# A third slot for the stream of weights inside two feed-forward loops: every third load goes into a buffer that another tile calls home

## The chip, the cores and the metric

The kernel runs on one core of one Trainium2 chip. TensorE (PE) multiplies matrices, ScalarE (ACT) and VectorE (DVE) do elementwise work, GpSimd (POOL) issues some of the transfers, SyncE (SP) issues the rest. The metric is the time of one execution on the device, in microseconds; a time given for a kernel is the median over several executions, and a profile is one further execution with the hardware profiler on.

## The reference, cut to what matters

The kernel computes one decoder layer on 512 tokens of width 1024 in float32: a feed-forward part, a mixing part (attention and a linear recurrence side by side), a second feed-forward part. Each is wrapped in a norm before and a norm behind.

```python
def swiglu(x, w_gate, w_up, w_down):
    return (jax.nn.silu(x @ w_gate) * (x @ w_up)) @ w_down

f = swiglu(rms_norm(h, ffn1_norm_pre[l]), ffn1_w_gate[l], ffn1_w_up[l], ffn1_w_down[l])
h = h + 0.5 * rms_norm(f, ffn1_norm_post[l])
u = rms_norm(h, mix_norm_pre[l])
...                                   # attention, recurrence, their gates
h = h + rms_norm(merged @ w_out[l], mix_norm_post[l])
f = swiglu(rms_norm(h, ffn2_norm_pre[l]), ffn2_w_gate[l], ffn2_w_up[l], ffn2_w_down[l])
h = h + 0.5 * rms_norm(f, ffn2_norm_post[l])
```

The inner width of both feed-forward parts is 2816, that is 22 parts of 128 columns. Only these two parts (called ffn1 and ffn2 below) are touched.

## The kernel before, in words

**Numbers in two halves.** A float32 product is made of three matmuls on a reduced type, fp32r. Every operand is first split into a high part, which ScalarE writes as a copy into fp32r (L278), and a low part, which VectorE makes as the difference (L279). So each piece of weights passes a load, a ScalarE copy and a VectorE subtraction before TensorE can use it. The three matmuls of a triple are high by high, high by low and low by high (L603 to L605 in the feed-forward products; L397 to L399 where the product is turned towards tokens; L783 to L785 in `down7`).

**The stream of weights.** All weights lie in device memory in the order of use. `raw_of` (L217 to L234) hands them out by key; at the first key of a group it allocates a tile `raw` of 128 x 2048 float32 (1 MB) and issues one load on SyncE (L224). The tiles have two buffers (tag `raw`, `bufs=2`), so a load can start only when the last reader of the load two before it is done. There are 118 groups, numbered from 0; the first eight are loaded by `fetch_start`, the other 110 by L224.

**A feed-forward part.** The 22 parts of columns are cut into five blocks (4, 4, 4, 4 and 6 parts). The first few parts are computed plainly. For every later part f there is a `prep` (function `w_forms`) and a `prod`. `w_forms` loads gate and up weights of f as one group, `gu`, makes sums of its quarters on VectorE (L579, L580, L581, L584) and splits them into the seven operands of a Strassen-like scheme. `prod` (functions `seven` and `product`) runs seven products of twelve matmuls in the order p1, p2, p6, p5, p7, p4, p3; copies of the results go out on ScalarE (L610, tile `c`), and VectorE forms `u` and `g` from them (L615). A `Silu` on ScalarE (L724) and a multiplication on VectorE (L725) give the activation, which `into` splits for later use. The `prep` of part f+1 stands in the program before the `prod` of part f.

**The way down.** After each of the blocks 1, 2 and 3 the product with the down weights is taken by `down7`, again with seven products; each of its 14 results is copied by ScalarE into one of eight slices of a tile `cs` (L789), and GpSimd issues 16 transfers (L791) that add these slices to the accumulator `facc` in SBUF. `d_forms` loads the two groups `dg` for it. Block 0 goes through `down` in two halves (L713 to L720, copies out at L717), and block 4 through `last_product` (L416), which also applies the gain row of the norm behind and takes sums of squares. In ffn1 `last_product` puts the weights of its second half into tiles of the tags `xf`, `e` and `tx`, in ffn2 into three further tiles called `wide` (shown as `big` in the profile).

**Homes.** Tiles of the feed-forward pool share buffers by tag, one buffer each for those named here. Tag `wd`: the activation of part 3 of block 0 (`act3`), which the two halves of `down(0, ...)` read; after ffn's loop, the gain rows of the norms (`gains`, L408, loaded by GpSimd at L409). Tag `tt`: sums of activations for `down7` (`sevens[a]["tt"]`, written in `into`, L725 and L687). Tag `e`: the other activations of block 0 (`act`), then the tile `cs` of each `down7`, then one operand of ffn1's `last_product`.

**What sets the order.** The program text gives dependences; a scheduler that works on its own estimate of times decides the order of the instructions on each engine. `tc.high_priority(offset=...)` lets it move the enclosed lines ahead by that many places: `AHEAD` (100) is round the loads and splits of weights, `EVAC` (200) round the copies out and the sums in `seven` and `down7`. On the chip each engine runs its own instructions in the order so decided and waits with semaphores for the others.

Of the kernel before, what the change touches and what calls it, by code (L numbers as in the profile page):

```python
# [10 lines left out]
F32 = mybir.dt.float32  # L11
# [5 lines left out]
P = 128  # L17
# [12 lines left out]
RAW_W = 2048  # L30
# [47 lines left out]
def part_blocks(a):  # L78

    return (FF_PARTS[a][1] - FF_PARTS[a][0]) // 2  # L80
# [62 lines left out]
def stream_groups():  # L143

    groups, cur, w = [], [], 0
    for key, width in stream_plan():
        if w + width > RAW_W or (cur and cur[0][0][0] == "start"):
            groups.append(cur)
            cur, w = [], 0
        cur.append((key, w, width))  # L150
        w += width
    groups.append(cur)
    return groups
# [12 lines left out]
def hybrid_layer(ctx: ExitStack, tc: tile.TileContext, xT: bass.AP, xN: bass.AP, wst: bass.AP,  # L166
# [6 lines left out]
    wpool = ctx.enter_context(tc.tile_pool(name="wpool", bufs=4))  # L173
# [24 lines left out]
    def fb(b, sl=slice(0, D)):  # L198
        return facc[:, 2 * b:2 * b + 2, :].rearrange("p k t -> p (k t)")[:, sl]
# [10 lines left out]
    DVE.memset(eps, EPS)  # L210


    groups = stream_groups()
    state = {"g": 0, "i": 0, "off": 0, "raw": None, "ahead": AHEAD}

    def raw_of(key):

        g, i = state["g"], state["i"]
        grp = groups[g]
        if i == 0:  # L220
            w = grp[-1][1] + grp[-1][2]
            raw = wpool.tile([P, RAW_W], F32, name="raw", tag="raw", bufs=2)
            src = bass.AP(tensor=wst.tensor, offset=wst.offset + state["off"], ap=[[w, P], [1, w]])
            nc.sync.dma_start(raw[:, :w], src)  # L224
            state["raw"] = raw
            state["off"] += w * P
        k, o, w = grp[i]
        assert k == key, (k, key)
        src = state["raw"][:, o:o + w]
        if i + 1 == len(grp):  # L230
            state["g"], state["i"] = g + 1, 0
        else:
            state["i"] = i + 1
        return src  # L234

    def fetch(key, slot=None, ahead=0):

        with tc.high_priority(offset=ahead if slot else state["ahead"]):
            src = raw_of(key)
            w = src.shape[-1]  # L240
            t = slot() if slot else w8() if w > 512 else w4()
            split(t[:, 0, :w], t[:, 1, :w], src)
            return t[:, 0, :w], t[:, 1, :w]
# [37 lines left out]
    def acc_ps():  # L281
        return psum.tile([P, T], F32, name="acc", tag="acc", bufs=5)

    def aux_ps():
        return psum.tile([P, T], F32, name="aux", tag="aux", bufs=3)

    def tmp(name):
        return tpool.tile([P, T], F32, name=name, tag="t")
# [17 lines left out]
    def gemm(ps, wt, x, sl=slice(0, T), n=None):  # L306
        n = n or x.n
        a, b = k128(wt[0], n), k128(wt[1], n)
        for k in range(n):
            mm3(ps, a[:, k, :], b[:, k, :], x.hi[k][:, sl], x.lo[k][:, sl], k == 0, k == n - 1)  # L310
# [50 lines left out]
    def warm(acc):  # L361
        d = cpool.tile([P, 1], F32, name="warm", tag="warm")
        ACT.activation(d, acc[:, 0:1], AF.Abs_reciprocal_sqrt, bias=eps, scale=1.0 / D)
# [23 lines left out]
    def square(src):  # L387

        q, t = tmp("sq"), stat()
        ACT.activation(q, src, AF.Square, accum_out=t)  # L390
        return t

    def tokens(ps, ws, x, b, fill=lambda: None):
        bl = slice(b * P, (b + 1) * P)
        for k in range(x.n):
            wh, wl = (w.rearrange("p (k c) -> p k c", k=2)[:, k % 2, :] for w in ws[k // 2])
            PE.matmul(ps, x.hi[k][:, bl], wh, start=k == 0, stop=False)  # L397
            PE.matmul(ps, x.hi[k][:, bl], wl, start=False, stop=False)  # L398
            PE.matmul(ps, x.lo[k][:, bl], wh, start=False, stop=k == x.n - 1)  # L399
            if k == x.n // 2 - 1:  # L400
                fill()
# [11 lines left out]
    def last_product(key, nk, x, added, grow, slots, block, fills={}, apart=False):  # L413


        sums = {}  # L416
        warm(eps)
        for half, fs in enumerate(FHALVES):
            ws = [fetch(key(half, kk), slots.pop(0) if half else None) for kk in range(nk)]
            for b in range(4):  # L420
                ps = acc_ps()
                tokens(ps, ws, x, b, fills.get((half, b), lambda: None))
                src, y = ps, fb(b, fs)
                if added:
                    DVE.tensor_add(y, ps, y)
                    src = y
                sums[b, half] = square(src)
                z = tmp("z") if apart and half else y
                DVE.tensor_mul(z, src, grow[:, fs])
                if half:  # L430
                    block(b, (sums[b, 0], sums[b, 1]), *([z] if apart else []))

    class Boundary:
# [7 lines left out]
        def block(self, b, sums):  # L441
            r = root(sums, self.f)
            DVE.scalar_tensor_tensor(hb(b), fb(b), r, hb(b), op0=ALU.mult, op1=ALU.add)
            nc.gpsimd.dma_start(self.kept[b], hb(b))
            r = root([square(hb(b, fs)) for fs in FHALVES], 1.0)
            us = []
            for fs in FHALVES:
                u = tmp("u")
                DVE.scalar_tensor_tensor(u, hb(b, fs), r, self.grow[:, fs], op0=ALU.mult, op1=ALU.mult)
                us.append(u)  # L450
            self.u[b] = us
# [68 lines left out]
    def tx_slot(pool, bufs=1):  # L520
        return pool.tile([P, 2, 4, HB], F32R, name="tx", tag="tx", bufs=bufs)
# [46 lines left out]

        return t, [early, middle, late]

    spool = [None]

    def w_forms(key):

# [58 lines left out]
    def ffn(n, x, r, forms_x, apool, pss):  # L633
# [26 lines left out]
        def part(a):  # L660
            his, los = zip(*(acts["at", f] for f in range(*FF_PARTS[a])))
            return Act(his, los)
# [48 lines left out]
        def down(a, half):  # L711
            ws = [fetch(("down", n, a, half, kk)) for kk in range(part_blocks(a))]
            for b in range(4):  # L713
                ps, y = acc_ps(), fb(b, FHALVES[half])
                tokens(ps, ws, part(a), b)
                if a == 0:
                    ACT.activation(y, ps, AF.Copy)  # L717
                else:
                    DVE.tensor_add(y, ps, y)

        def prod(f, w):
            g, u = tmp("g"), tmp("u")
            seven(t, w, aux_ps()[:, :HB], [g[:, h] for h in HALVES], [u[:, h] for h in HALVES])
            ACT.activation(g, g, AF.Silu)  # L724
            into(f, lambda dst: DVE.scalar_tensor_tensor(dst, g, -1.0, u, op0=ALU.mult, op1=ALU.mult))  # L725
# [78 lines left out]
        for ev in ffn_order(n):  # L804
            if ev[0] == "std":
                j = ev[1]
                while len(pss) < 2 * j + 2:
                    pss.append(acc_ps())
                    gemm(pss[-1], fetch(keys[len(pss) - 1]), x)
                std_out(pss[2 * j], pss[2 * j + 1], j)  # L810
                if j < len(steps):
                    steps[j]()
            elif ev[0] == "prep":
                forms[ev[1]] = w_forms(("gu", n, ev[1]))
            elif ev[0] == "prepd":
                forms["d"] = d_forms(ev[1])
            elif ev[0] == "down":
                down(ev[1], ev[2])
            elif ev[0] == "down7":
                down7(ev[1], *forms.pop("d"))  # L820
            else:
                prod(ev[1], forms.pop(ev[1]))
        a = len(FF_PARTS) - 1
        return lambda half, kk: ("down", n, a, half, kk), part_blocks(a), part(a)

# [6 lines left out]
    def spare(pool):  # L832

        def of(t):
            return t[:, 0:4, :].rearrange("p (s k) t -> p s (k t)", s=2)

        return {"e": lambda: of(pool.tile([P, 8, T], F32R, name="act", tag="e", bufs=1)),
                "tt": lambda: of(pool.tile([P, 4, T], F32R, name="act", tag="tt", bufs=1)),
                "xf": lambda: of(pool.tile([P, 4, T], F32R, name="xf", tag="xf", bufs=4)),
                "tx": lambda: tx_slot(pool).rearrange("p s k t -> p s (k t)")}  # L840
# [14 lines left out]
    for k in range(KC):  # L855
        wh, wl, raw = wts[k]
# [9 lines left out]


    end1 = ffn(1, u1, r1, x_forms("g1a", r1, ap1), ap1, pss)
    new_h()
    for b in range(4):  # L870
# [10 lines left out]
            bd1.turn(b - 2)  # L881

    last_product(*end1, True, grow1, [spare(ap1)[i] for i in ("xf", "e", "tx")], block1)
    ff1.close()


    with ExitStack() as mx:
        tpl = mx.enter_context(tc.tile_pool(name="attn_out", bufs=1))
        apool_cm = tc.tile_pool(name="attention", bufs=1)
        apool = apool_cm.__enter__()  # L890
# [207 lines left out]
        for c in range(0, KC, 2):  # L1098
            g, u = tmp("g"), tmp("u")
# [308 lines left out]
```

## Time and profile before

| what | value |
|---|---|
| median of 3 executions | 1270.91 us (1269.04 to 1272.77) |
| the profiled execution's own time | 1275.29 us |
| its span in the profile | 1273.5 us |
| mean granted clock of TensorE | 0.987 |
| TensorE busy | 1230.8 us, 97% of the span |
| VectorE busy | 971.4 us, 76% |
| ScalarE busy | 735.1 us, 58% |
| loads at L224 | 110 of up to 1 MB, median 4.8 us from issue to landing |

A row of the timeline gives an instruction's start, its duration, engine, line and operation, written tile <- read tiles, and in brackets how long the engine sat idle before it and what released it. A row of waits gives the total time waited, the number of times and the longest. A row of a stretch gives, after the stretch's bounds and length, the busy time of PE, PE's weight loads, DVE, ACT and POOL with the number of instructions, then the granted clock, the mean busy share of the 16 DMA engines and GB/s. Lines below are of the kernel before.

In time, ffn1 lies in the first 350 us of the span, and ffn2's feed-forward loop in the last 340.

### The profile page before, as it was taken

Reading aid. Unit: us, or ns where it says so; the run is one execution under the profiler, and the core shown is the slowest. Engines: PE = TensorE matmul, PEld = TensorE weight load, DVE = VectorE, ACT = ScalarE, POOL = GpSimd, SP = SyncE. Lnnn points to the kernel's source line nnn. Section 1 sums busy time; section 2 is a strip of 40 time slices with the busy share of each in tenths; the row PEclk is TensorE's granted clock in tenths of the full one; section 3 lists DMA queues with packets and bytes.
Section 4 is the critical chain, followed back from the end, with each engine's and each line's share of the span. In section 5 each row is a group of like instructions: output and inputs, shape, how many; then the busy total and the mean of one; then the engine's idle time right before and its main releaser. Section 6 shows DMA issues by size and latency. Waiting matters only on the chain.

```text
span 1273.5 us, 19380 instructions
## 1 busy us (share of the span) xinstructions
PE 1230.8 (97%) x7676; PEld 1114.4 (88%) x7676; DVE 971.4 (76%) x1521; ACT 735.1 (58%) x1214; POOL 113.4 (9%) x153
## 2 busy tenths in 40 slices
PE   9999999999999999999999999999999999989887
PEld 8889888989777899999988887888998989888886
DVE  7969697878577488888575888854885879787855
ACT  7546656565455455666543797634664575756442
POOL 0000314030002000000000000000100031313000
PEclk9999999999899999999999999999999999999889
DMA  6233859584535122222242222225533386858631
GB/s 237 100 105 111 198 150 209 140 199 134 196 116 158 66 108 80 96 77 98 98 167 99 94 74 97 102 97 182 161 122 115 103 204 153 202 140 187 157 133 66
DMA packets 42075, 169.72 MB, mean 133 GB/s; under 512 B 4608, under 2 KB 7808, under 8 KB 27904
## 3 DMA queue, kind: packets, MB, share of 16 engines
q1 hardware_dynamic: 20016, 122.86, 28.0%
q0 software_dynamic: 21968, 45.62, 16.5%
q8 instruction: 60, 0.98, 0.3%
q14 instruction: 31, 0.25, 0.1%
HBM read 129.67 MB, written 6.29 MB: 107 GB/s over the span
## 4 chain that ended last, share of the span: by engine, by line
PE 73%; DVE 12%; DMA 8%; ACT 5%; issue 2%; DVEq 0%; SPq 0%; ACTq 0%
PE acc L603 8%; PE acc L604 8%; PE acc L605 8%; DMA raw<-in_w 8%; PE acc L291 6%; PE acc L292 6%; PE acc L293 6%; DVE w L279 4%; PE acc L397 3%; PE acc L399 3%; PE acc L398 3%; PE acc L783 2%; PE acc L784 2%; PE acc L785 2%; PE aux L603 2%; PE aux L604 2%
## 5 line engine op out<-in xcount | busy, mean ns | idle before, releaser
L279 DVE TENSOR_TENSOR w<-raw,w 128x1024 fp32r<-128x1024 f32 (+1 forms) x279 | 304.0, 1094 | 105.5 <-ACT w L278 93.1
L278 ACT ACTIVATE w<-raw 128x1024 fp32r<-128x1024 f32 (+1 forms) x279 | 265.5, 954 | 155.4 <-PE acc L293 48.3
L603 PE MATMUL acc<-big,w 128*128 128x256 f32 x896 | 254.7, 284 | 0.6 <-ACT c L610 0.6
L604 PE MATMUL acc<-big,w 128*128 128x256 f32 x896 | 254.6, 284 | 0.0
L605 PE MATMUL acc<-big,w 128*128 128x256 f32 x896 | 254.1, 284 | 0.0
L603 PEld LDWEIGHTS acc<-big,w 128*128 128x128 f32 x896 | 172.1, 192 | 1.4 <-ACT c L610 0.9
L604 PEld LDWEIGHTS acc<-big,w 128*128 128x128 f32 x896 | 172.0, 192 | 0.4
L605 PEld LDWEIGHTS acc<-big,w 128*128 128x128 f32 x896 | 172.0, 192 | 0.0
L603 PE MATMUL acc<-tx,w 128*128 128x256 f32 x272 | 80.0, 294 | 24.1 <-ACT c L610 23.9
L791 POOL DMA_DIRECT2D facc<-cs x96 | 82.0, 872 | 152.7 <-ACT cs L789 75.8
L610 ACT ACTIVATE c<-acc 128x256 f32<-128x256 f32 x172 | 65.0, 378 | 49.8 <-PE acc L605 46.1
L603 PE MATMUL aux<-big,w 128*128 128x256 f32 x288 | 83.2, 289 | 0.0
L604 PE MATMUL aux<-big,w 128*128 128x256 f32 x288 | 83.1, 288 | 0.0
L605 PE MATMUL aux<-big,w 128*128 128x256 f32 x288 | 83.0, 288 | 0.0
L605 PE MATMUL acc<-tx,w 128*128 128x256 f32 x272 | 78.7, 289 | 0.0
L604 PE MATMUL acc<-tx,w 128*128 128x256 f32 x272 | 78.4, 288 | 0.0
L603 PEld LDWEIGHTS acc<-tx,w 128*128 128x128 f32 x272 | 53.5, 197 | 26.5 <-ACT c L610 26.5
L291 PE MATMUL acc<-big,w 128*128 128x512 f32 x192 | 74.7, 389 | 0.0
L292 PE MATMUL acc<-big,w 128*128 128x512 f32 x192 | 74.7, 389 | 0.0
L293 PE MATMUL acc<-big,w 128*128 128x512 f32 x192 | 74.7, 389 | 0.0
L579 DVE TENSOR_TENSOR s<-raw 128x512 f32<-128x512 f32 x52 | 35.9, 690 | 47.0 <-DMA raw<-in_w 46.9
L279 DVE TENSOR_TENSOR w<-s,w 128x1024 fp32r<-128x1024 f32 x52 | 63.5, 1221 | 2.8 <-ACT w L278 2.7
(352 smaller groups left out, 2982.7 us busy)
## 6 DMA issues: line engine op xcount, KB each, us to landing
raw<-in_w SPq DMA_DIRECT2D x110, 1024.0 KB, 4.8
facc<-cs POOLq DMA_DIRECT2D x96, 256.0 KB, 6.7
raw<-raw POOLq DMA_DIRECT2D x6, 512.0 KB, 4.4
big<-xf POOLq DMA_DIRECT2D x6, 512.0 KB, 4.5
gains<-in_rows POOLq DMA_DIRECT2D x5, 512.0 KB, 7.4
h<-in_x SPq DMA_DIRECT2D x8, 256.0 KB, 5.2
h<-in_xn POOLq DMA_DIRECT2D x4, 512.0 KB, 5.5
kept_m<-h POOLq DMA_DIRECT2D x4, 512.0 KB, 2.9
```

The lines of the kernel that those rows point to most:

```text
L278: ACT.activation(dh, src, AF.Copy)
L279: DVE.tensor_sub(dl, src, dh.bitcast(F32))
L291: PE.matmul(ps, wh, xh, start=first, stop=False)
L292: PE.matmul(ps, wh, xl, start=False, stop=False)
L293: PE.matmul(ps, wl, xh, start=False, stop=last)
L397: PE.matmul(ps, x.hi[k][:, bl], wh, start=k == 0, stop=False)
L398: PE.matmul(ps, x.hi[k][:, bl], wl, start=False, stop=False)
L603: PE.matmul(ps, wh, xh, start=start and k == 0, stop=False, skip_group_check=True)
L604: PE.matmul(ps, wh, xl, start=False, stop=False, skip_group_check=True)
L605: PE.matmul(ps, wl, xh, start=False, stop=k == 3, skip_group_check=True)
L610: ACT.activation(c, ps, AF.Copy)
L791: nc.gpsimd.dma_start(fb(o + i, FHALVES[half]), c, accum_op=ALU.add)
```

## The change

Group g of the stream is loaded into a third place when g divided by 3 leaves 2 and such a place is set. From the end of `down(0, 1)` on, the place is the buffer of tag `wd`; after the loop over ffn's events it is the buffer of tag `tt`; after ffn1's `last_product` it is none again, and `down(0, 0)` of ffn2 sets it to none too. The groups so placed are 14, 17, 20, 23, 26, 29, 32 and 35 (tag `wd`) and 38 (tag `tt`) in ffn1, and 92, 95, 98, 101, 104, 107, 110 and 113 (tag `wd`) and 116 (tag `tt`) in ffn2. Group 14 is `gu` of part 6, group 92 is `gu` of part 5. The list `spool`, of which only the first place was used before (the pool of the tag `s`), now has a second place and is made earlier.

```diff
--- before.py
+++ after.py
@@ -210,6 +210,7 @@
     DVE.memset(eps, EPS)
 
 
+    spool = [None, None]
     groups = stream_groups()
     state = {"g": 0, "i": 0, "off": 0, "raw": None, "ahead": AHEAD}
 
@@ -219,7 +220,10 @@
         grp = groups[g]
         if i == 0:
             w = grp[-1][1] + grp[-1][2]
-            raw = wpool.tile([P, RAW_W], F32, name="raw", tag="raw", bufs=2)
+            if spool[1] is not None and g % 3 == 2:
+                raw = spool[1][0].tile([P, RAW_W], F32, name="raw", tag=spool[1][1], bufs=1)
+            else:
+                raw = wpool.tile([P, RAW_W], F32, name="raw", tag="raw", bufs=2)
             src = bass.AP(tensor=wst.tensor, offset=wst.offset + state["off"], ap=[[w, P], [1, w]])
             nc.sync.dma_start(raw[:, :w], src)
             state["raw"] = raw
@@ -568,7 +572,6 @@
 
         return t, [early, middle, late]
 
-    spool = [None]
 
     def w_forms(key):
 
@@ -816,10 +819,12 @@
                 forms["d"] = d_forms(ev[1])
             elif ev[0] == "down":
                 down(ev[1], ev[2])
+                spool[1] = (apool, "wd") if ev[2] else None
             elif ev[0] == "down7":
                 down7(ev[1], *forms.pop("d"))
             else:
                 prod(ev[1], forms.pop(ev[1]))
+        spool[1] = apool, "tt"
         a = len(FF_PARTS) - 1
         return lambda half, kk: ("down", n, a, half, kk), part_blocks(a), part(a)
 
@@ -881,6 +886,7 @@
             bd1.turn(b - 2)
 
     last_product(*end1, True, grow1, [spare(ap1)[i] for i in ("xf", "e", "tx")], block1)
+    spool[1] = None
     ff1.close()
```

The loads are the same in number and size; the activation of part 3, the gain rows and the sums of activations keep their tags.

## The prediction, on record before the changed kernel ran

> **What bounds the kernel now.** I read the page's busy times first, then what ended TensorE's idle time, then the timeline at each of TensorE's gaps, back through ScalarE and VectorE to the load.
>
> ```profile
> span 1273.5 us, 19380 instructions
> PE 1230.8 (97%) x7676; PEld 1114.4 (88%) x7676; DVE 971.4 (76%) x1521; ACT 735.1 (58%) x1214; POOL 113.4 (9%) x153
> raw<-in_w SPq DMA_DIRECT2D x110, 1024.0 KB, 4.8
> facc<-cs POOLq DMA_DIRECT2D x96, 256.0 KB, 6.7
> PE acc L603 <- ACT c L610: 24.5, 11, 3.7
> PE acc L397 <- ACT xf L278: 6.3, 2, 3.2
> DVE s L579 <- DMA raw<-in_w: 46.9, 28, 3.8
> ```
>
> TensorE is the bound: 1230.8 of 1273.5 us. Two groups hold 24.5 + 6.3 = 30.8 us of its 42.7 idle: thirteen gaps, all in the feed-forward loops. The profiled run took 1275.29 us, 4.4 above the median 1270.91; the sum is made against 1275.29 and carried to the median at the end.
>
> What makes a typical gap, after a `down7` (times are starts; brackets give idle time and releaser):
>
> ```profile
> 148.52 0.33 SPq L224 DMA_DIRECT2D raw<-in_w  x1
> DMA to landing us min/median/max: 7.6/7.6/7.6
> 156.17 0.69 DVE L579 TENSOR_TENSOR s<-raw 128x512 f32<-128x512 f32 x1 [3.40 <-DMA raw<-in_w]
> 161.49 0.63 ACT L724 ACTIVATE g<-g 128x512 f32<-128x512 f32 x1 [4.18 <-DVE g L615]
> 162.45 0.39 PE L603 MATMUL acc<-tx,w 128*128 128x256 f32 x1 [3.07 <-ACT c L610]
> 163.00:165.00 2.00, 2.00 (x19) 2.00 (x18) 2.00 (x5) 1.57 (x3) 0.00 (x0) 1.00 0.97 233
> 97.24 0.39 PE L603 MATMUL acc<-tx,w 128*128 128x256 f32 x1 [1.48 <-ACT c L610]
> 289.77 0.39 PE L603 MATMUL acc<-tx,w 128*128 128x256 f32 x1 [2.98 <-ACT c L610]
> 290.00:296.00 6.00, 6.00 (x39) 6.00 (x39) 4.41 (x8) 3.55 (x7) 0.00 (x0) 0.72 0.97 234
> ```
>
> A load that is issued at 148.52 and lands 7.6 us later holds VectorE's first sum of the next weights for 3.40 us. Behind it in VectorE's order stand the sums of the running product; behind these ScalarE's activation, then its copy, then TensorE. In the rows of stretches (busy time by engine, then granted clock, DMA share, GB/s) the mean clock is 1.00 behind this gap of 3.07, and 0.72 over the 6 us behind that of 2.98: 6 x 0.28 = 1.7 us lost. So a gap of this size sometimes also brings slow clock.
>
> [...]
>
> **The change part by part.** Loads are the same 110 and the same bytes, and every engine issues the same instructions; what moves is their order, slots and waits.
>
> *Ring of three, inner products (gaps after `down7`).* With two slots load n waits for the last reader of n−2. With every third load elsewhere it waits, in the built program, for that of n−2 or n−3, and since the loads go in order on SyncE, load n+1 takes the instant that load n had (148.52 brings the load after). VectorE's sums of that load are moved forward with it, to the same place ahead of the running product's sums. So VectorE waits again about 3.4 us, and the gap stays: seven gaps at 0, between −2 each if the load came early enough and +1 if more transfers collide. Only at 97.24 is there no `down7` beside it; there load 15 comes before its sums are due, and I take its 1.48 gap away: **−1.4** (0 to −1.5).
>
> *ffn1, third `down7`.* The load of the last half of the final `down` (load 38, slot `tt`) needs no ring slot and stands in the built SyncE order ahead of load 32, so it is issued at about 260. Its first split (ScalarE, L278 → `act`, into the buffers of tag `e`) now stands right behind the copy that began at 278.90. The tag `e` is also where `down7` keeps `cs`, the sources of its accumulating transfers, so that split waits for the last eight of these.
>
> ```profile
> 260.47 0.33 SPq L224 DMA_DIRECT2D raw<-in_w  x1
> 278.90 0.37 ACT L610 ACTIVATE c<-acc 128x256 f32<-128x256 f32 x1
> 279.91 1.05 ACT L278 ACTIVATE w<-raw 128x1024 fp32r<-128x1024 f32 x1
> 287.23 1.22 DVE L279 TENSOR_TENSOR w<-raw,w 128x1024 fp32r<-128x1024 f32 x1
> 288.81 0.63 ACT L724 ACTIVATE g<-g 128x512 f32<-128x512 f32 x1 [4.18 <-DVE g L615]
> 284.87 0.87 POOL L791 DMA_DIRECT2D facc<-cs  x1 [5.24 <-ACT w L278]
> DMA to landing us min/median/max: 3.5/3.5/3.5
> 288.71 0.85 POOL L791 DMA_DIRECT2D facc<-cs  x1 [0.48 <-issue]
> DMA to landing us min/median/max: 9.2/9.2/9.2
> 283.00:291.00 8.00, 5.03 (x41) 4.82 (x40) 7.28 (x12) 3.25 (x6) 3.41 (x4) 0.99 1.02 206
> ```
>
> The last of those transfers is issued at 288.71 and lands 9.2 later, at 297.9. Queued behind the split on ScalarE are the copies of the running product, the next product's weight splits and the activation, so TensorE stops from about 282 on. With the landing at R the chain on is three splits of 1.05 and two copies of 0.37 on ScalarE (3.9), then on VectorE a low part of 1.22, a sum of 0.69 and a further low part of 1.22, then the activation 0.63 and a copy 0.37: R + 8.0 for the matmul that began at 289.77 (the half-width sums of the running product I take to lie within these). R is 297.9 at most as long as the queue of transfers is what it was; with ScalarE and VectorE held, later loads are not issued and the transfers come quicker, 292 at the least (issue 288.71 and 3.5, the landing of the one issued at 284.87). The DMA share is 1.02 there, full, with the same number of loads, so I take R = 295: 303.0, which is 13.2 late, less the 1.7 of half clock already behind that gap: **+11.5** (8.6 at R = 292, 16 at 298 with a longer half clock).
>
> *ffn2, first third-slot load (the weights `gu`, part 5).* The slot is the buffer of tag `wd`, in which the fourth part's activation lies until the last matmul of `down(0, half 1)` has read it.
>
> ```profile
> 954.19 0.33 SPq L224 DMA_DIRECT2D raw<-in_w  x1
> 980.07 0.39 PE L399 MATMUL acc<-w,act 128*128 128x512 f32 x1
> 980.29 0.28 PE L603 MATMUL acc<-big,w 128*128 128x256 f32 x1
> 994.33 0.39 PE L603 MATMUL acc<-tx,w 128*128 128x256 f32 x1 [0.93 <-ACT c L610]
> ```
>
> Before, the load went out at 954.19, and the product that needs it followed the last reader without a gap, at 980.29. Now the load goes out after 980.07: 980.2 + 4.8 (landing) + 1.05 (split) = 986.1 for its first matmul, a gap of 5.9. In the built order six sums (three for this load, three for the next; 0.69 each, as at 156.17) stand before its low part (1.22) on VectorE, which the third matmul of each group of three reads: 985.0 + 4.1 + 1.2, about 990. TensorE does six matmuls and stops again: 9.0 in all, allowing for these. A gap of that size brings half clock (+2.2, between the 1.7 above and twice that); the gap at 994.33 goes (−0.9). **+10.3** (8 to 12.5). The same wait stands in ffn1, but there the load is of part 6 and reaches TensorE's use some 10 us after the slot is free, so it is hidden.
>
> *Gains of the norm.* They share `wd`, and are now loaded after the slot's last load instead of at 83.14, beside the last loads of ffn1.
>
> ```profile
> 83.14 1.20 POOL L409 DMA_DIRECT2D gains<-in_rows  x2 [82.70 <-PE acc L399]
> gains<-in_rows POOLq DMA_DIRECT2D x5, 512.0 KB, 7.4
> q1 hardware_dynamic: 20016, 122.86, 28.0%
> 332.35 1.06 ACT L278 ACTIVATE tx<-raw 128x1024 fp32r<-128x1024 f32 x1 [5.71 <-DMA raw<-in_w]
> 335.99 0.79 PE L397 MATMUL acc<-w,xf 128*128 128x512 f32 x1 [3.07 <-ACT xf L278]
> ```
>
> At 332.35 ScalarE waits for a load, and the gap of 3.07 at 335.99 follows. In the new order a split on the next load still stands ahead of the activation; two transfers of 512 KB more take part, by bytes one load. A load takes all 16 engines for 28.0% of 1273.5 us / 122.86 MB, some 2.9 us for 1 MB; I take 2.4 at most, since the weights go on moving beside it, and half of that: **+1.2** (0 to 2.4). For ffn2 the gains are needed some 30 us after the slot is free: 0.
>
> *ffn2, third `down7`.* Here too the early load of `tt` adds 1 MB to full queues: **+2** (0 to 3, by the same 2.9 us). Its split goes to another tile than `cs`, so nothing like +11.5 is added.
>
> *End of ffn2.*
>
> ```profile
> 1214.78 0.33 SPq L224 DMA_DIRECT2D raw<-in_w  x1
> 1221.98 0.33 SPq L224 DMA_DIRECT2D raw<-in_w  x1
> 1229.96 1.06 ACT L278 ACTIVATE big<-raw 128x1024 fp32r<-128x1024 f32 x1 [4.88 <-DMA raw<-in_w]
> 1233.59 0.80 PE L397 MATMUL acc<-w,xf 128*128 128x512 f32 x1 [3.25 <-ACT xf L278]
> 1233.00:1241.00 8.00, 7.41 (x20) 5.85 (x21) 3.00 (x4) 1.27 (x3) 0.00 (x0) 0.58 0.00 1
> ```
>
> The last load goes out at 1214.78 instead of 1221.98 and has landed before ScalarE comes to it. The gap of 3.25 falls to about 0.8 (what is late next is the activation's own chain) and the slow clock behind it (8 x 0.42 = 3.4 lost) goes: **−5.9** (0 to −6).
>
> Sum: −1.4 + 11.5 + 10.3 + 1.2 + 2 − 5.9 = **+17.7**, so 1293.0 for the profiled run; against the median 1270.91 + 17.7 = **1288.6**. I give 1288.
>
> **The rivals.**
> *Faster: the third slot takes the load waits out.* If VectorE no longer waits at L579, the gaps behind the six `down7` go (two behind the first): at the 3.07 and 2.98 shown, seven times about 3, some 20 us, with 1.7 of slow clock behind some. The point that decides is whether a load lands before VectorE reaches its first sum, 3.4 us sooner than now. For it: 46.9 us of VectorE's idle is that wait, and the slot's release is a real bound on SyncE. Against it: the sums move forward with the load. With −21 there, −7 at 97 and the end, and the losses of +11.5 and +10.3 halved by such slack, the sum is −17: 1254. [...]
> *About the same.* The transfers of `cs` have landed earlier (R near 284, as for a landing of 3.5 had they all been issued by 280), so the split at 279 costs nothing, and the loss in ffn2 (+10.3) is paid by the end's −5.9, −1.4 and a `down7` gap or two: 1271. Against it: the last of the transfers is only issued at 288.71.
> *Slower by much more.* R at 298, half clock of 3.4 behind both stops, no gain at the end: 16 + 12.5 + 3.2 = +31.7, or 1302.
>
> **How the numbers follow.** A change under 0.3% (3.8 us) is not told from none. My forecast, with both stops, 72%; the larger loss 10%; one of the two stops missing (1276 to 1280) 8%; about the same 5%; faster 5%. So slower 0.90, same 0.05, faster 0.05. The range goes from 1275 (one stop missing, the end's gain whole) to 1300 (upper ends of both stops); its ends leave the other cases out, some 15%.
>
> **What would show it.** Right: at about 980 a TensorE gap near 6 us with the load issued behind the last L399 and a shorter one after it; at 282 to 303 a ScalarE wait of some 14 us at an L278 split into `act`, released by `facc<-cs`; L579 still waiting about 3 us after each `down7`; no gap at 97 nor at the end of ffn2. Wrong: if that split waits for little, I misjudged R (−11); if L579's total falls from 46.9 to under 20, the ring's release was the bound and the faster rival holds; if the last gap stays, add 5.9.

## The result, and the profile after

The changed kernel takes 1290.05 us (median of 3 executions, 1289.66 to 1292.53) against 1270.91 before. The ratio is 1.0156, 95% interval 1.0125 to 1.0187: slower by 19.1 us. Forecast was 1288 in a range of 1275 to 1300. The profiled execution has a span of 1290.8 us, 17.3 more than the one of before.

The page of the changed kernel and what ended TensorE's, VectorE's and ScalarE's idle time (name of the waiting instruction <- what it waited for: total us, times, longest):

```profile
PE 1234.8 (96%) x7676; PEld 1118.8 (87%) x7676; DVE 968.5 (75%) x1521; ACT 735.6 (57%) x1214; POOL 114.4 (9%) x153
...
PE acc L606 <- ACT c L613: 23.5, 10, 4.8
PE acc L606 <- ACT w L282: 6.0, 1, 6.0
PE acc L401 <- ACT xf L282: 4.2, 1, 4.2
...
DVE s L582 <- DMA raw<-in_w: 58.0, 19, 23.0
...
ACT cs L792 <- DMA facc<-cs: 14.6, 13, 5.5
```

TensorE's busy time is 4 us longer (mean granted clock 0.980, against 0.987 before); the rest of the growth is waiting. Two waits are of new kinds: 9.1 us behind ScalarE's copy, which stands behind the 13.1 us that the split into `act` waits for the transfers out of `cs`, and 6.0 us directly on a weight split. The first group keeps nearly its 24.5 us of before, so a third slot has not emptied it. In the kernel after, lines up to L222 are one higher, then three to six.

Where the time went can be read from instructions that both kernels run once each: the multiplication behind `Silu`, L725 before and L728 after, and the last use of `facc` in the tail. Before, then after, from VectorE's timelines:

```profile
247.17 0.69 DVE L725 SCALAR_TENSOR_TENSOR u<-g,u 128x512 f32<-128x512 f32 x1 [0.83 <-ACT g L724]
300.73 0.69 DVE L725 SCALAR_TENSOR_TENSOR u<-g,u 128x512 f32<-128x512 f32 x1
961.22 0.68 DVE L725 SCALAR_TENSOR_TENSOR tt<-g,u 128x512 f32<-128x512 f32 x1
1066.48 0.69 DVE L725 SCALAR_TENSOR_TENSOR u<-g,u 128x512 f32<-128x512 f32 x1
1218.39 0.69 DVE L725 SCALAR_TENSOR_TENSOR u<-g,u 128x512 f32<-128x512 f32 x1 [0.70 <-ACT g L724]
1266.26 0.68 DVE L425 TENSOR_TENSOR facc<-acc,facc 128x512 f32<-128x512 f32 x1
```

```profile
246.69 0.68 DVE L728 SCALAR_TENSOR_TENSOR u<-g,u 128x512 f32<-128x512 f32 x1
314.40 0.69 DVE L728 SCALAR_TENSOR_TENSOR u<-g,u 128x512 f32<-128x512 f32 x1
974.12 0.69 DVE L728 SCALAR_TENSOR_TENSOR tt<-g,u 128x512 f32<-128x512 f32 x1 [0.70 <-ACT g L727]
1090.11 0.69 DVE L728 SCALAR_TENSOR_TENSOR u<-g,u 128x512 f32<-128x512 f32 x1
1241.93 0.69 DVE L728 SCALAR_TENSOR_TENSOR u<-g,u 128x512 f32<-128x512 f32 x1 [0.70 <-ACT g L727]
1283.49 0.68 DVE L429 TENSOR_TENSOR facc<-acc,facc 128x512 f32<-128x512 f32 x1
```

The difference of each pair is the lag: −0.5, +13.7, +12.9, +23.6, +23.5, +17.2. TensorE's own lags at these places, taken by pairing the nth matmul of L603 with the nth of L606 (1456 in either trace) and so for the other lines, agree within 0.7 us. Between neighbours:

| stretch | measured | forecast terms |
|---|---|---|
| ffn1 up to its third `down7` | −0.5 | −1.4 (gap at 97), the `down7` gaps 0 |
| ffn1's third `down7` | +14.2 | +11.5 |
| from there through the mixing part | −0.8 | +1.2 (end of ffn1, gains) |
| start of ffn2's loop, with its first `down7` | +10.7 | +10.3 |
| rest of ffn2's loop | −0.1 | +2 |
| end of ffn2 | −6.3 | −5.9 |
| sum | +17.2 | +17.7 |

The third `down7` of ffn1, in the order of time, from the timelines of TensorE, GpSimd and ScalarE of the kernel after (the landing line belongs to the GpSimd row above it):

```profile
280.44 0.58 PE L606 MATMUL acc<-tx,w 128*128 128x256 f32 x1 [4.76 <-ACT c L613]
...
292.61 0.86 POOL L794 DMA_DIRECT2D facc<-cs  x1 [0.42 <-issue]
DMA to landing us min/median/max: 4.1/4.1/4.1
...
296.89 1.06 ACT L282 ACTIVATE act<-raw 128x1024 fp32r<-128x1024 f32 x1 [13.09 <-DMA facc<-cs]
297.85 0.36 ACT L613 ACTIVATE c<-aux 128x256 f32<-128x256 f32 x1
298.27 0.58 PE L606 MATMUL aux<-big,w 128*128 128x256 f32 x1 [9.12 <-ACT c L613]
303.80 0.38 ACT L613 ACTIVATE c<-acc 128x256 f32<-128x256 f32 x1
```

The last `cs` transfer lands at 292.61 + 4.1 = 296.7, the split that waited 13.09 us starts at 296.89, and the copy behind it frees TensorE at 298.27. The gap of 4.76 at 280.44, ahead of all this, was not in the forecast.

The start of ffn2's loop (SyncE, VectorE, TensorE):

```profile
993.51 0.39 PE L403 MATMUL acc<-w,act 128*128 128x512 f32 x1
993.92 0.33 SPq L228 DMA_DIRECT2D raw<-in_w  x1
998.74 1.29 DVE L582 TENSOR_TENSOR s<-raw 128x512 f32<-128x512 f32 x2 [23.01 <-DMA raw<-in_w]
999.91 0.58 PE L606 MATMUL acc<-big,w 128*128 128x256 f32 x1 [6.01 <-ACT w L282]
1001.84 0.58 PE L606 MATMUL aux<-big,w 128*128 128x256 f32 x1 [0.71 <-ACT w L282]
1003.63 0.58 PE L608 MATMUL acc<-big,w 128*128 128x256 f32 x1 [0.99 <-DVE w L283]
```

The load goes out 0.4 us after the start of the last matmul that reads `act3`, lands 4.8 us later, and TensorE, which ran on without a gap before, stands for 6.01 us, for 0.71 behind the next split, at 1001.84, and for 0.99 again, at 1003.63, before the low part is there. The end of ffn2 has no gap of TensorE in the trace any more; its last load went out at 1238.33, which less the lag of 23.5 is 1214.8 on the clock of before:

```profile
1238.33 0.33 SPq L228 DMA_DIRECT2D raw<-in_w  x1
```

### The profile page after: what moved, and what is told of

Its sections match the earlier page's. It is cut to its first block, busy times and chain, and to the rows that moved or that the text cites. A ratio compares the mean times of both kernels' runs of the same rounds, so it can differ in the third digit from the quotient of the medians.

```text
span 1290.8 us, 19406 instructions
## 1 busy us (share of the span) xinstructions
PE 1234.8 (96%) x7676; PEld 1118.8 (87%) x7676; DVE 968.5 (75%) x1521; ACT 735.6 (57%) x1214; POOL 114.4 (9%) x153
## 4 chain that ended last, share of the span: by engine, by line
PE 73%; DVE 11%; DMA 7%; ACT 5%; issue 3%; POOL 1%; DVEq 0%; ACTq 0%; POOLq 0%
PE acc L606 9%; PE acc L608 9%; PE acc L607 9%; PE acc L295 6%; PE acc L296 5%; PE acc L297 5%; DMA raw<-in_w 5%; DVE w L283 4%; PE acc L403 3%; PE acc L401 3%; PE acc L402 3%; PE aux L606 2%; PE aux L608 2%; PE aux L607 2%; DMA facc<-cs 2%
## 5 line engine op out<-in xcount | busy, mean ns | idle before, releaser
L606 PE MATMUL acc<-big,w 128*128 128x256 f32 x896 | 256.4, 286 | 6.0 <-ACT w L282 6.0
L606 PEld LDWEIGHTS acc<-big,w 128*128 128x128 f32 x896 | 174.0, 194 | 7.1 <-ACT w L282 6.4
L606 PE MATMUL acc<-tx,w 128*128 128x256 f32 x272 | 80.5, 296 | 23.5 <-ACT c L613 23.5
L606 PE MATMUL aux<-big,w 128*128 128x256 f32 x288 | 84.7, 294 | 9.8 <-ACT c L613 9.1
L607 PE MATMUL aux<-big,w 128*128 128x256 f32 x288 | 84.1, 292 | 0.0
L608 PE MATMUL aux<-big,w 128*128 128x256 f32 x288 | 83.9, 291 | 0.0
L606 PEld LDWEIGHTS acc<-tx,w 128*128 128x128 f32 x272 | 53.9, 198 | 25.6 <-ACT c L613 25.6
L606 PEld LDWEIGHTS aux<-big,w 128*128 128x128 f32 x288 | 58.0, 201 | 10.5 <-ACT c L613 9.5
```

Source lines behind the costliest of these rows:

```text
L606: PE.matmul(ps, wh, xh, start=start and k == 0, stop=False, skip_group_check=True)
L607: PE.matmul(ps, wh, xl, start=False, stop=False, skip_group_check=True)
L608: PE.matmul(ps, wl, xh, start=False, stop=k == 3, skip_group_check=True)
```

## The experiments

Each time is a median over executions on one chip, beside the kernel before on the same chip (1270.96 to 1272.38 us in these groups). Single executions of one kernel spread by 5 us and, in `late_wd` and `big_late`, by up to 9 us either way, so differences of less than 2 us between medians are not read, and those of 2 to 4 with care. Diffs are against the changed kernel if nothing else is said.

**Is the loss in two places?** First `tt` is not used.

```diff
-        spool[1] = apool, "tt"
+        spool[1] = None
```

> Third slot in wd only, none for the last group of each feed-forward part. Theory A (the prices come from places: +14.5 us at ffn1's third down7 because the early load's split holds ScalarE, +9.7 at ffn2's first third-slot load, -6.9 at the end of ffn2 because the last load takes an earlier slot): the 14.5 go, and the 6.9 come back with them, so 1290.05 - 14.5 + 6.9 = about 1282.5; no ScalarE wait of 13 us on facc<-cs, a gap of 9 us on TensorE missing near 298, a gap of about 3.3 back at the end of ffn2. Rival B (the loss is spread over the loops by more loads in flight): within 3 us of 1290.

Measured: 1282.47 us, ratio to before 1.0103 (1.0073 to 1.0133). This is theory A's number. No wait on `facc<-cs` stands among ScalarE's splits, and the end of ffn2 has its gap again, as the timeline of TensorE in this kernel shows beside what is left at the third `down7`:

```profile
287.18 0.39 PE L606 MATMUL acc<-tx,w 128*128 128x256 f32 x1 [0.98 <-ACT c L613]
1241.61 0.79 PE L401 MATMUL acc<-w,xf 128*128 128x512 f32 x1 [2.54 <-ACT xf L282]
```

Then the slot in ffn2 is opened one product later, so that group 92 stays in the ring.

```diff
-                spool[1] = (apool, "wd") if ev[2] else None
+                spool[1] = (apool, "wd") if ev[2] and n == 1 else None
...
                 prod(ev[1], forms.pop(ev[1]))
+                spool[1] = apool, "wd"
```

> As the changed kernel, but in ffn2 the third slot is opened only after the first product behind down(0), so that the load of gu 5 stays in the ring and no load waits for the last reader of act3. Theory A: the 9.7 us of that place go, all else stays: 1280.4; no TensorE gap of 6 us near 1000. Rival B (spread over the loops): 1290 within 3. Rival C (the wait only moves to the next group that gets the slot): 1285 to 1290, with a gap of some us behind the next product.

Measured: 1278.52 us, ratio 1.0062 (1.003 to 1.0095), 11.5 less than the changed kernel where 9.7 was expected. The wait of 23 us is gone from VectorE's list, and no gap near 1000 takes its place:

```profile
DVE s L582 <- DMA raw<-in_w: 40.9, 19, 4.5
```

So the loss is not spread over the loops (rival B), and it does not move to the next group (rival C).

**The block at ffn1's third `down7`: place in the queue, or contention?** The early load stays, only the operand that lived in tag `e` gets another home.

```diff
-    last_product(*end1, True, grow1, [spare(ap1)[i] for i in ("xf", "e", "tx")], block1)
+    last_product(*end1, True, grow1, [spare(ap1)["xf"], lambda: big([P, 2, 1024]), spare(ap1)["tx"]], block1)
```

> As the changed kernel, with the operand of ffn1's last product that had its home in tag e put into a big tile instead; the early load stays. Theory A (position in ScalarE's queue: the split waits for the cs transfers): the 13 us ScalarE wait and the 9.1 us TensorE gap go, between -9 and -14.5: 1275.5 to 1281. Rival D (contention: the early load makes the cs transfers late, and these stop TensorE by themselves): 1287 or more, with the gaps of 4.8 and more behind the third down7 still there.

Measured: 1279.63 us, ratio 1.008 (1.005 to 1.011), 10.4 less than the changed kernel. TensorE at the same place:

```profile
278.12 0.57 PE L606 MATMUL acc<-tx,w 128*128 128x256 f32 x1 [3.27 <-ACT c L613]
```

The 9.12 us are gone with the wait (the longest gap there is 0.60), and a gap of 3.27 stays where 4.76 was. So both hold: the place in ScalarE's queue is some 10 us of the loss, and the early load beside the transfers is the rest, since with `no_tt`, which has no early load, the gaps of that place are under 1 us.

The same stop without the ring: `tt` in both parts, nothing in `wd`.

```diff
-                spool[1] = (apool, "wd") if ev[2] else None
+                spool[1] = None
```

> No slot in wd, tt in both parts: the ScalarE stop without the ring. Theory A: 1271.6 + 14.5 - 6.9 = 1279.2, with a ScalarE wait of some 13 us on facc<-cs near 297. If the stop needs the wd loads beside it: 1270 or less.

Measured: 1282.39 us, ratio 1.008 (1.0062 to 1.0097); 3 us more than expected. The stop stands as before, so it does not need the loads in `wd`:

```profile
298.00 1.06 ACT L282 ACTIVATE act<-raw 128x1024 fp32r<-128x1024 f32 x1 [13.08 <-DMA facc<-cs]
```

**Both places mended.** `wd` late in ffn2 (as in `late_wd`) and

```diff
-        spool[1] = apool, "tt"
+        spool[1] = (apool, "tt") if n == 2 else None
```

> wd opened late in ffn2, tt used in ffn2 only: both losing places taken out, the end's gain kept. Theory A: 1290.05 - 14.5 - 9.7 = 1265.9, that is 5 us faster than before. Rival B (spread over the loops) 1285 or more. Rival E (the slot brings nothing of its own, gains and losses of the places cancel otherwise): 1271 within 2.

Measured: 1265.09 us, ratio 0.9962 (0.9937 to 0.9986): faster than before. With the early load kept in ffn1 instead, its operand in the big tile (the edits of `late_wd` and `big_slot` together):

> Both places as in the changed kernel, wd late in ffn2, the operand of tag e in a big tile: the early load of ffn1 stays, its split does not block. Theory A with the loss of big_slot: 1279.6 - 9.7 = 1269.9, that is some 4 to 5 us above late_no_tt1, the price of the early load beside the cs transfers in the third down7 of ffn1. Rival G (the early load costs nothing once its split is out of the way): 1265.

Measured: 1273.59 us, ratio 1.0009 (0.9989 to 1.0029), 8.5 above `late_no_tt1` by the medians and 6.0 by the ratios to before. The early load is not free with its split out of the way; rival G falls. The traces put less on it than the medians do. Its gap in `big_late` is this, and `late_no_tt1` has none of 0.9 or more between 223 and 331:

```profile
281.44 0.39 PE L606 MATMUL acc<-tx,w 128*128 128x256 f32 x1 [4.27 <-ACT c L613]
```

Counted matmul by matmul, the profiled `big_late` loses 4.7 us on the profiled `late_no_tt1` in ffn1's third `down7`, as theory A had it; of the 9.1 us between their spans, 3.2 stand ahead of the early load and 1.2 behind that place. Between `big_slot` and `no_tt`, which also differ in the early load, it is 3.5 in the same place. In both pairs the operand's home differs too, and no run takes the two apart.

**What is the ring worth, and what the end?** Two kernels with one of the gains each: `late_wd` with no `tt`, and `tt` in ffn2 only with no `wd`. Their only edits are the lines already shown.

> The slot in wd alone, opened late in ffn2, none in tt: what the ring of three is worth inside the loops. Theory A (the waits behind the down7 stay, since each load takes the instant of the one before and its sums move forward with it; only the gap at 97 goes): late_no_tt1 plus the 6.9 us of the end, 1272.0, no difference from before within 2. Rival F (the ring itself makes the gain of late_no_tt1): 1263 to 1267.

> No slot in wd; tt for the last group but one of ffn2 alone. Theory A: the end's 6.9 us, less 0 to 2 for the earlier load in the third down7 of ffn2: 1264.7 to 1266.7, no TensorE gap near 1233. Rival F (the ring makes the gain): 1270 to 1272.

Measured: 1268.95 us (0.998, 0.9963 to 0.9997) and 1271.41 us (0.9997, 0.9982 to 1.0012). The first is 2.5 faster than before. That is 3 us below theory A's 1272.0 and 2 above the upper end of rival F, so it decides for neither. The second misses theory A by some 5 us and lies where rival F had it. In its profile the gap near 1233 is gone as expected, but gaps of 2.47, 0.71 and 3.48 us, against one of 3.66 before, stand in and behind the third `down7` of ffn2; the largest two are:

```profile
1175.43 0.39 PE L606 MATMUL acc<-tx,w 128*128 128x256 f32 x1 [2.47 <-ACT c L613]
1200.60 0.39 PE L606 MATMUL acc<-tx,w 128*128 128x256 f32 x1 [3.48 <-ACT c L613]
```

By TensorE's lags that profile loses 1.1 us in the third `down7`, 1.7 in the second, ahead of the early load, and gains 6.2 at the end. So the trace shows the end's gain as theory A had it; why the median is no better than before is not shown, and the spread of executions may be part of it. The two together bring 6.3 (1271.4 to 1265.09) and singly 2.5 and 0; no run isolates why.

**Why the gaps behind `down7` stay.** The prediction said that VectorE's sums move forward with the load. In this test the first three sums of a `gu` group are bound behind the last elementwise instruction of the product traced before it; nothing else is changed from `late_no_tt1`.

```diff
-            DVE.tensor_add(s12[:, 1, :], u0, u1)
-            DVE.tensor_add(s12[:, 0, :], s12[:, 1, :], g0)
-            DVE.tensor_add(u0, u0, g0)
+            with tc.issue_after(state["tail"].ins) if state.get("tail") is not None else ExitStack():
+                DVE.tensor_add(s12[:, 1, :], u0, u1)
+                DVE.tensor_add(s12[:, 0, :], s12[:, 1, :], g0)
+                DVE.tensor_add(u0, u0, g0)
...
-            into(f, lambda dst: DVE.scalar_tensor_tensor(dst, g, -1.0, u, op0=ALU.mult, op1=ALU.mult))
+            def last(dst):
+                state["tail"] = DVE.scalar_tensor_tensor(dst, g, -1.0, u, op0=ALU.mult, op1=ALU.mult)
+
+            into(f, last)
```

> late_no_tt1 with one more thing: the first three sums of each gu group on VectorE are ordered behind the last elementwise instruction (L728 there) of the product traced before them, so a load that is late can no longer hold the running product's u and g sums. Theory A (the gaps behind the down7 come from VectorE's order, not from a lack of slots: with the third slot the load lies ready, and only its sums stand too early): the five gaps of 1.9 to 4.5 us and part of the slow clock behind them go: 1265.1 less 10 to 20, 1245 to 1255. Rival H (the loads are late in themselves beside the cs transfers, and the wait only moves from the sums of u and g to the next product): 1262 to 1268. Rival I (the forms are now made too late for the next product): over 1268.

And the same edit on the kernel before, with two slots:

> The kernel before, two slots, with the same order of the sums. Theory A: here the load itself comes after the running product's sums are due, ScalarE still waits for it in front of its activation (2 us and more behind each down7), so the gaps shrink but stay: 1271.4 less 2 to 8. Rival J (the order alone does it, no slot is needed): as far below before as order_3slots is below late_no_tt1. Rival I (forms too late): slower than before by 5 or more.

Measured: 1247.8 us with three slots (ratio to before 0.9809, 0.9785 to 0.9834) and 1258.58 us with two (0.9897, 0.9872 to 0.9923). The first is inside theory A's range. Timeline of VectorE and waits in the three-slot kernel:

```profile
157.77 0.69 DVE L730 SCALAR_TENSOR_TENSOR tt<-g,u 128x512 f32<-128x512 f32 x1 [0.70 <-ACT g L728]
158.38 0.69 DVE L583 TENSOR_TENSOR s<-raw 128x512 f32<-128x512 f32 x1
...
PE acc L607 <- ACT c L614: 8.4, 6, 2.6
...
DVE s L583 <- DMA raw<-in_w: 12.2, 8, 2.1
...
ACT w L282 <- DMA raw<-in_w: 10.5, 5, 3.6
```

The sum now follows the product's last instruction and does not wait. TensorE's waits behind the copies fall to 8.4 us, from 20.3 in `late_no_tt1` and 24.5 before. What is left is mostly of another kind. The largest are gaps of 2.58 at 148.31 and 2.59 at 1157.13, and there the copy stands on ScalarE behind copies into `cs`, which wait for a slice that a transfer still reads:

```profile
143.91 0.60 ACT L796 ACTIVATE cs<-acc 128x512 f32<-128x512 f32 x1 [1.64 <-DMA facc<-cs]
148.31 0.39 PE L607 MATMUL acc<-tx,w 128*128 128x256 f32 x1 [2.58 <-ACT c L614]
```

With two slots VectorE waits 21.7 us for the load at its first sum, against 12.2 with three, and ScalarE's splits wait more too:

```profile
PE acc L604 <- ACT c L611: 11.6, 21, 1.6
...
DVE s L580 <- DMA raw<-in_w: 21.7, 14, 2.7
...
ACT w L278 <- DMA raw<-in_w: 39.5, 23, 3.7
```

My expectation for two slots was a gain of 2 to 8, and it is 12.8 to 13.8 by the two medians it may be set against: most of the gain is the order alone, as rival J had it. But the slot is worth something once the order is right, 10.8 us between the medians of the two kernels. How much of it is the end of ffn2 was asked by taking `tt` out of the three-slot kernel:

> order_3slots without tt: what the tt place at the end of ffn2 is worth where the ring works. Theory A: the end's gap and its slow clock come back, 1247.8 + 4 to 7 = 1252 to 1255, the rest of the 10.8 us between order_2slots and order_3slots being the ring's in the loops. Rival L (the ring is worth nothing in the loops): 1257 to 1259.

Measured: 1252.02 us (0.9835, 0.9813 to 0.9856). By the medians 4.2 of the 10.8 are the end and some 6.6 the ring in the loops; by the ratios to before, 3.3 and 7.9. The traces do not show where in the loops. The profiled spans are 1252.8 us with two slots, 1251.8 here and 1247.8 with the end, the first from the fastest execution of its kernel and the second from the slowest, and by TensorE's lags the ring brings nothing in ffn1 and 2.0 us in ffn2's loop. So the size of the ring's part stays open. Last, the same idea on ScalarE, on top of `order_3slots`: a split that waits for a load stands ahead of the `Silu` at the ends of both parts, so the splits of the second half are bound behind it.

```diff
-            split(t[:, 0, :w], t[:, 1, :w], src)
+            with tc.issue_after(state["silu"].ins) if slot else ExitStack():
+                split(t[:, 0, :w], t[:, 1, :w], src)
...
-            ACT.activation(g, g, AF.Silu)
+            state["silu"] = ACT.activation(g, g, AF.Silu)
```

> order_3slots, and the splits of the second half of each feed-forward part's last product are ordered behind the last Silu on ScalarE. Theory A (the same fault at ffn1's end: a split that waits for its load stands in front of the activation): the gap of 3.9 us near 327 and the slow clock behind it (1.7) go: 1247.8 - 5 = about 1243. Rival K (the second half's weights are then late themselves): 1246 to 1250.

Measured: 1242.12 us, ratio to before 0.9761 (0.9743 to 0.978). The gap of 3.91 at 326.89 in `order_3slots` is gone. This beats both kernels of the case, and its page has TensorE busy for nearly the whole span of 1239.6 us:

```profile
PE 1221.8 (99%) x7676; PEld 1105.7 (89%) x7676; DVE 968.1 (78%) x1521; ACT 734.5 (59%) x1214; POOL 114.5 (9%) x153
```

## Why the prediction was right, point by point

*The gap at 97* went, as predicted: TensorE's lag falls by 1.7 us there. Not all of it is to be seen at 247, since other things moved too. In `tt_only` and `tt2_only`, which leave `wd` alone, the gap is there (1.76 and 1.84).

*The gaps behind `down7`.* Nearly right in the sum, but only half right in the mechanism. Of seven gaps the one at 162 went, those at 149 and 225 stayed, as the timelines of ScalarE and TensorE in the changed kernel have them, and slow clock came where there was none (last section).

```profile
143.83 0.60 ACT L792 ACTIVATE cs<-acc 128x512 f32<-128x512 f32 x1 [1.34 <-DMA facc<-cs]
148.56 0.39 PE L606 MATMUL acc<-tx,w 128*128 128x256 f32 x1 [2.81 <-ACT c L613]
...
224.64 0.39 PE L606 MATMUL acc<-tx,w 128*128 128x256 f32 x1 [3.19 <-ACT c L613]
```

The prediction had one kind of gap in mind: VectorE's sum waits for its load ahead of the running product's sums. Six of the seven gaps before are so, all but that at 149.04. In the changed kernel this holds for those at 224.64, 1080.66 and 1143.78 (3.19, 1.30 and 3.38). At 148.56, 1069.03 and 1199.18 (2.81, 1.97 and 4.56) and at 280.44 the copy that TensorE needs stands on ScalarE behind the copies into `cs` and splits of weights. Those copies wait for the transfers out of `cs` for 14.6 us in 13 waits, against 7.3 in 7 before, and one of them for 5.48 at 1193.43, ahead of the gap at 1199.18. Leaving out ffn1's third `down7`, the gaps sum to 17.2 us, against 18.0 before: the first kind fell from 15.7 to 7.9, the second rose from 2.3 to 9.3. That the sum stayed at 0 is luck in part, since the prediction had no term for the second kind.

`order_3slots` shows the first kind, for binding the sums takes the gap at 225 away and leaves the one at 148, while the third slot alone (`wd_only_late`) gave 2.5 us. The rival "faster" failed at the point I named for it only in part: VectorE's waits for the load at its first sum did fall, from 46.9 us to 35.0 without the 23.0 of ffn2's start, but they stayed at several `down7`s (3.29 at 218.36, 3.72 at 1137.49), and ScalarE's waits took the place of others. In these runs it was order first (12.8 us with two slots) and buffers second (10.8 more by the medians, the end of ffn2 among them).

*ffn1's third `down7`.* Right: ScalarE waits 13.09 us in the split into `act`, for the transfers out of `cs`, and `big_slot` takes 10.4 us back by another home for that tile. R was taken as 295 and measured at 296.9, by two errors of which one hides part of the other: the last transfer went out at 292.61 instead of 288.71, and it landed in 4.1 us where R = 295 allowed 6.3. R + 8.0 would be 304.9, and the matmul that stood at 289.77 is here:

```profile
305.03 0.28 PE L606 MATMUL acc<-tx,w 128*128 128x256 f32 x1
```

That is 15.3 late, where the working said 13.2, and 1.9 of the difference is R. The agreement is not the chain alone. The copy ahead of this matmul starts at 303.80, a little sooner than worked out, and TensorE had no idle time left there: it ran again from 298.27, on matmuls at a granted clock of 0.54 (300 to 304). What the term lacked is that the copies into `cs`, and with them the transfers, are late themselves, which the gap of 4.76 at 280.44 shows too. I gave the early load no price of its own in that place ("with the same number of loads"); with its split out of the way it is 3.5 to 4.7 us there by the traces (`big_slot` against `no_tt`, `big_late` against `late_no_tt1`).

*ffn2's first third-slot load.* Right in place and size: 6.01 for the 5.9 that I worked out, smaller stops behind it than the 3 us I had (0.71 and 0.99; the matmuls between ran at a granted clock of 0.50, from 999 to 1005, and used up that time), +10.7 for +10.3; `late_wd` took back 11.5 by the medians. The stops are 7.7 instead of 9.0. By TensorE's lags, 13.6 ahead of the stops and 23.7 at the matmul that starts at 1006.15, the slow clock cost some 2.4 there, where I had 2.2, and from there through the first `down7` the lag grows by a further 0.6, where I had −0.9 for the gap at 994.33; so the misses cancel.

*End of ffn1, gains.* The term was +1.2 and −0.8 came: 2 us off, and the wrong sign. The gap grew as feared, from 3.07 to 4.22, but less slow clock followed. The growth goes with the moved load of the gains: in the four kernels where it is still issued at 83 to 84 (`tt_only`, `tt2_only`, `order_2slots` and the one before) the gap is 3.02 to 3.40, in those with `wd`, `order_3slots_end` aside, 3.31 to 4.34. Rows of ten microseconds behind the gap, before and after (mean clock in the third column from the end):

```profile
335.00:345.00 10.00, 9.01 (x27) 7.18 (x28) 5.22 (x7) 3.03 (x6) 0.00 (x0) 0.66 0.29 105
```

```profile
350.00:360.00 10.00, 9.20 (x33) 7.44 (x34) 3.55 (x6) 2.08 (x5) 0.00 (x0) 0.83 0.00 0
```

3.4 us lost there before, 1.7 after. I had no term for the clock at that place.

*Third `down7` of ffn2.* +2 was forecast and −0.1 measured for the whole rest of the loop, so this term was too large here, or something else in the loop paid for it: the gap there did grow, from 3.66 to 4.56.

*End of ffn2.* Right: no gap, −6.3 for −5.9.

The total came out within some 2 us also because the 2.7 us that the term of ffn1's third `down7` was short and the two small terms that did not come (1.2 and 2) offset each other.

## What to carry to other kernels

A further buffer for a stream moves what reads the stream forward too: with the third slot VectorE still waited 3.29 and 3.72 us at the first sums at 218.36 and 1137.49. If the built order lets the readers run ahead on an engine that works it off in order (on ScalarE the copy behind the split that waited 13.09 us started only at 297.85), the wait only travels with them: look at what is queued behind the waiting instruction, and bind the late reader behind that work before buying a buffer, which brought 12.8 us here with two slots. A buffer lent from another tile brings that tile's last reader as a new condition (the stop of 6.01 us in ffn2), and a load that comes free of the ring can be hoisted so far that its consumer blocks an engine on an unrelated transfer (the 13.09 us in ffn1); check both ends of each borrowed home, the first use and the one after the last.

## What the runs showed of the hardware that was not expected

Where the clock fell, it stood at 0.50: from 291 to 294 and from 1233 to 1239 in the kernel before, which is the half clock of the prediction, and from 999 to 1005 in the changed one. In these runs the length of the gap alone does not decide whether it falls. Behind the gap of 2.81 at 148.56 in the changed kernel the mean clock over 6 us is 0.72, that is 1.7 us lost. As much is lost behind a gap of only 1.84 at 98.54 in `tt2_only` (second row: 5.4 us at 0.68), and nothing behind one of 3.16 at 328.20 in `order_2slots` (third row):

```profile
149.00:155.00 6.00, 6.00 (x40) 6.00 (x39) 3.76 (x6) 3.02 (x6) 1.05 (x2) 0.72 0.97 237
98.60:104.00 5.40, 5.40 (x33) 5.40 (x34) 4.98 (x9) 2.86 (x6) 0.00 (x0) 0.68 0.08 32
328.30:334.30 6.00, 6.00 (x27) 4.93 (x28) 4.04 (x6) 2.17 (x5) 0.00 (x0) 1.00 0.49 176
```

What else decides, no run here isolates.

And the last five transfers of `cs` landed in 3.4 to 4.1 us while ScalarE and VectorE stood still, against a median of 8.5 for the last four before, the very last in 9.2. The loads of weights were missing there: their queue moved 0.22 MB from 284 to 297 us, against 1.05 MB in the same stretch before. That a stop empties the queue and so shortens itself is read from these rows; no run isolates it.
